# A mixed attention layer on one core: the first unit of every two in three softmax pairs is transposed by VectorE's 32x32 squares and a trip through DRAM

## The chip, the core and the metric

The kernel runs on one core of one Trainium2 chip. A core has five engines with an instruction queue each: PE (TensorE, matmuls, with its weight loads shown as PEld), DVE (VectorE), ACT (ScalarE), POOL (GpSimd) and SP (SyncE, which here only issues DMAs). Each engine works through its own queue in order; an instruction whose inputs are not there holds everything behind it on that engine. The metric is the device time of one execution in microseconds (us). Data lie in SBUF (128 partitions), matmuls write to PSUM banks, and DRAM holds inputs, outputs and a few scratch arrays.

## What is computed

A layer of a sequence model, 1024 positions by 1024 channels in float32: a layer norm with a modulation computed from a conditioning vector, one input projection, two groups of eight attention heads (stick-breaking and softmax with a forget gate), a gate, an output projection, and a residual with a second layer norm. The softmax group is the one that the change touches:

```python
s = jnp.einsum('bhqd,bhkd->bhqk', q, k) * scale
s = s + (f_q[..., :, None] - f_k[..., None, :])
s = jnp.where(causal, s, -jnp.inf)
p = jax.nn.softmax(s, axis=-1)
out = jnp.einsum('bhqk,bhkd->bhqd', p, v)
...
y = jnp.concatenate([y_fox * silu(fg), y_sb * silu(sg)], axis=-1) @ w_out
x = layer_norm(alpha * x + gate * y) * ln_g + ln_b
```

Queries go in blocks of 128; block i sees keys 0 to 128(i+1). The f_k are running sums of log forget gates, one row of 1024 for each head.

## The kernel before

**Precision.** Matmul operands are kept as a high part (rounded) and a low part (the rest), and a product is made of several matmuls (high by high, high by low, low by high). So each operand has a cast that makes the high part and a subtraction that makes the low part.

**Pairs and units.** The 16 heads go in 8 pairs p: 0 to 3 stick-breaking, 4 to 7 softmax. A unit (p, h, i) is one block of 128 queries of head h of pair p. Pairs 4 to 6 run head 0 and then head 1, each with i = 7 down to 0, so an odd i comes first of every two that share a product. Unit names in the profile and in the instruction order: `a_0_7` is the attention tile of head 0, i = 7 of the pair then running, `S_0_7` its scores, `T_0_7_0` and `T_0_7_1` its transposes for blocks 0 to 3 and 4 to 7, `pv_0_3` the product of units 7 and 6 with the values, `pt_4_0_3_0` a transposed operand of pair 4, head 0, pair of units 3, blocks 0 to 3.

**One softmax unit.** PE makes the scores S in the one S tile of PSUM (L427, L428). DVE adds the forget row `fb` and takes the row maximum in one pass, writing tile `a` (L434), which frees S. ACT takes the exponential and its row sum `l` (L440), DVE the reciprocal of `l` (L441), POOL scales `a` by it (L442). Two units later (LAG = 2) `att_transpose` turns the unit's 128x128 blocks on PE into a PSUM tile T (L478, i + 1 blocks), ACT casts T into the high part of `pt` (L480) and DVE subtracts for the low part (L481). One turn after the second unit of a pair of units has been transposed, `att_pv` makes the product on PE, 2i + 2 matmuls for odd i (L493): first all with the high part, then those with the low part, blocks 0 to 3 ahead of blocks 4 to 7. ACT, DVE and POOL then copy, add and gate the result (L512 to L514), and SP writes it to `y_dr` (L522).

**Beside it.** Between the attention matmuls of a pair, PE runs the projections of later pairs (L270 to L272, and values L327 to L329). Their weights come by SP from DRAM (L121) and are split on POOL: cast L125, subtraction L126 (`whi`, `wlo`). The output weights go the same way in pairs 4 to 6 (L123, then L125, L126), are written to `wo_dr` by SP (L830, L831), and are read back near the end (`woh`, `wol`, L821, L822), as is the gated output (`yr`, L859). Forget rows of 1024, the same on all partitions, come by ACT's DMA queue (`fb`, L391). Tiles `a` and `fb` share a pool of six SBUF buffers ("att").

**What sets the order.** PE's order is the order of the program text, written by hand: for each step k of the main loop the scores of unit k, some projection steps, a product that is ready, the transposes of unit k - 2, more projection steps. The order on ACT, DVE, POOL and SP is made by the scheduler at build time from its own estimate of times. The helper `through_dram` and the names `on_dma`, `quartered` and `squares` exist only after the change.

Of the kernel before, what the change touches and what calls it, by code (L numbers as in the profile page):

```python
# [13 lines left out]
P = 128  # L14
# [13 lines left out]
def tile_hybrid_layer(  # L28
# [82 lines left out]
    f_dr = dr.tile([8, SEQ], F32, tag="f_dr", name="f_dr")  # L111

# [132 lines left out]
    def evac_k(p, ch, acc, kst, klo, heads):  # L245
        s = slice(ch * 512, ch * 512 + 512)
        for h in heads:
            r = slice(h * HD, h * HD + HD)
            o = slice((1 - h) * HD, (1 - h) * HD + HD)
            first = nc.scalar.copy(kst[h][r, s], acc[r, :])  # L250
            kf = kst[h].bitcast(F32)
            nc.sync.dma_start(kf[o, s], kf[r, s])
            if p not in CASTS_FIRST:
                last = nc.vector.tensor_tensor(klo[r, s], acc[r, :], kf[r, s], op=ALU.subtract)
        if p in CASTS_FIRST:
            for h in heads:
                r = slice(h * HD, h * HD + HD)
                last = nc.vector.tensor_tensor(klo[r, s], acc[r, :], kst[h].bitcast(F32)[r, s], op=ALU.subtract)  # L258
        return first, last
# [106 lines left out]
    def forget_rows(lf):  # L366
# [17 lines left out]
        nc.sync.dma_start(f_dr.rearrange("h (t p) -> (h t) p", p=P), fr)  # L384
# [22 lines left out]
    def att_causal(u):  # L407
        p, h, i = u
        if p >= 4:
            f = fb[2 * (p - 4) + h]  # L410
            dg = slice(i * P, i * P + P)
            nc.vector.tensor_tensor(f[:, dg], f[:, dg], ps_causal[0][:, :P] if ps_causal else causal, op=ALU.add)

    def att_scores(u, following):
# [4 lines left out]
        w = ke // ns  # L419
        qs = slice(i * P, i * P + P)  # L420
# [3 lines left out]
        S = s_tile(f"S_{p}_{h}_{i}")  # L424
        for s in range(ns):
            ks = slice(s * w, s * w + w)
            nc.tensor.matmul(S[:, s, :w], qst[p][h][:, qs], kst[p][h][:, ks], start=True, stop=False)  # L427
            nc.tensor.matmul(S[:, s, :w], z, klo[p][:, ks], start=False, stop=True)  # L428
        v3 = lambda a: a[:, :ke].rearrange("p (a b) -> p a b", a=ns)
        if p >= 4:  # L430
# [3 lines left out]
            rows = nc.vector.tensor_tensor_reduce(out=v3(a), in0=S[:, :ns, :w], in1=v3(f),  # L434
# [7 lines left out]
            nc.gpsimd.tensor_scalar(a[:, :ke], a[:, :ke], l, 1.0, op0=ALU.mult, op1=ALU.mult)  # L442
            st_w[u] = a
        else:
# [17 lines left out]
            nc.gpsimd.memset(be[:, ke - 1:ke], 0.0)  # L462
            st_w[u] = be

    def att_transpose(u):
        p, h, i = u
        a = st_w.pop(u)
        j, qo = i // 2, (i % 2) * P
        for g in range((i // 4) + 1):
            n = min(4, i + 1 - 4 * g)  # L470
            if (p, h, j, g) not in st_pt:
                st_pt[p, h, j, g] = [pt_tile(x, f"pt{x}_{p}_{h}_{j}_{g}", F32R, [P, 4, 256])
                                     for x in range(2)]
            hi, lo = st_pt[p, h, j, g]
            tp = t_tile(f"T_{p}_{h}_{i}_{g}")
            for b in range(n):
                kb = 4 * g + b
                nc.tensor.transpose(tp[:, b * P:(b + 1) * P], a[:, kb * P:(kb + 1) * P], ident)  # L478
            t3 = tp[:, :n * P].rearrange("p (a b) -> p a b", a=n)
            nc.scalar.copy(hi[:, :n, qo:qo + P], t3)  # L480
            nc.vector.tensor_tensor(lo[:, :n, qo:qo + P], t3, hi.bitcast(F32)[:, :n, qo:qo + P],  # L481
                                    op=ALU.subtract)
# [521 lines left out]
    for k in range(len(units) + LAG + 1):  # L1004
        if k < len(units):
# [13 lines left out]
            if 4 <= p < NPAIR - 1 and i == 0:  # L1019
                load_fb(2 * (p - 4) + h + 2)  # L1020
# [3 lines left out]
        if LAG <= k < len(units) + LAG:  # L1024
            u = units[k - LAG]
            att_transpose(u)
            seen.add(u)
            if (u[0], u[1], u[2] ^ 1) in seen:
# [76 lines left out]
```

## Time and profile before

| | |
|---|---|
| time, 3 runs | 685.13 us median (685.02 to 685.16) |
| the profiled execution | 685.25 us, span 683.5 us |
| granted TensorE clock | 0.999 |
| pairs 4 to 6 | about 349 to 559 us of the span |
| DMA moved | 81.60 MB |

The profile gives, for each engine, the time in which it was busy, and the chain of work that ended last, followed back from the end. Groups of instructions are given by line, engine, operation, output and inputs, with count, busy time, and mean ns of one after the bar. A window's row gives the busy time of each engine in a stretch of the span, then the granted clock, the share of the DMA engines and GB/s. A row of the timeline is start, duration, engine, line, operation, and in brackets the idle time just before it and what ended that. In the window views a row like `x16` is a run of 16 instructions. Matmuls overlap in PE's pipeline, so their rows are longer than the step from one to the next.

### The profile page before, as it was taken

Reading aid. Unit: us, or ns where it says so; the run is one execution under the profiler, and the core shown is the slowest. Engines: PE = TensorE matmul, PEld = TensorE weight load, DVE = VectorE, ACT = ScalarE, POOL = GpSimd, SP = SyncE. Lnnn points to the kernel's source line nnn. Section 1 sums busy time; section 2 is a strip of 40 time slices with the busy share of each in tenths; the row PEclk is TensorE's granted clock in tenths of the full one; section 3 lists DMA queues with packets and bytes.
Section 4 is the critical chain, followed back from the end, with each engine's and each line's share of the span. In section 5 each row is a group of like instructions: output and inputs, shape, how many; then the busy total and the mean of one; then the engine's idle time right before and its main releaser. Section 6 shows DMA issues by size and latency. Waiting matters only on the chain.

```text
span 683.5 us, 11770 instructions
## 1 busy us (share of the span) xinstructions
PE 667.2 (98%) x4021; PEld 587.2 (86%) x4021; DVE 450.6 (66%) x914; ACT 382.0 (56%) x861; POOL 427.7 (63%) x558
## 2 busy tenths in 40 slices
PE   5999999999999999999999999999999999999995
PEld 4789898888998888889988888899988889888885
DVE  6785368867666667676675665765566677774645
ACT  5668357856567666566675564655565667531000
POOL 5558977756348566556388896877584364665411
PEclk9999999999999999999999999999999999999999
DMA  9966231112102121122144563453341298143301
GB/s 338 410 236 233 82 105 44 41 29 60 29 9 86 27 57 54 37 55 55 55 131 136 172 176 121 143 166 129 101 150 40 72 327 318 58 162 118 123 31 62
DMA packets 45036, 81.60 MB, mean 119 GB/s; under 512 B 5232, under 2 KB 18864, under 8 KB 44976
## 3 DMA queue, kind: packets, MB, share of 16 engines
q1 hardware_dynamic: 43536, 76.63, 33.8%
q10 hardware_dynamic: 1440, 4.21, 2.2%
q8 instruction: 32, 0.52, 0.3%
q14 instruction: 28, 0.23, 0.1%
HBM read 60.34 MB, written 16.29 MB: 112 GB/s over the span
## 4 chain that ended last, share of the span: by engine, by line
PE 94%; DMA 3%; DVE 2%; ACT 0%; issue 0%; POOL 0%; DVEq 0%
PE m L270 10%; PE m L272 10%; PE m L271 10%; PE pv L493 10%; PE T L478 9%; PE S L428 5%; PE S L427 5%; PE o L884 4%; PE o L882 4%; PE o L883 4%; PE v L327 4%; PE v L328 4%; PE v L329 4%; DMA raws<-in_w_qkg_dram 2%; PE st_late L589 1%; PE st_q L589 1%
## 5 line engine op out<-in xcount | busy, mean ns | idle before, releaser
L270 PE MATMUL m<-uh,whi 128*128 128x512 f32 x304 | 126.4, 416 | 0.0
L272 PE MATMUL m<-uh,wlo 128*128 128x512 f32 x304 | 119.7, 394 | 0.0
L271 PE MATMUL m<-ul,whi 128*128 128x512 f32 x304 | 119.7, 394 | 0.0
L481 DVE TENSOR_TENSOR pt<-T,pt 128x512 fp32r<-128x512 f32 (+2 forms) x192 | 100.5, 550 | 17.5 <-ACT pt L480 16.5
L461 POOL TENSOR_TENSOR be<-be,kp 128x127 f32<-128x127 f32 (+3 forms) x64 | 77.2, 1207 | 33.1 <-DVE kp L457 23.5
L480 ACT CAST pt<-T 128x512 fp32r<-128x512 f32 (+2 forms) x192 | 85.8, 480 | 16.1 <-PE T L478 12.5
L453 DVE TENSOR_TENSOR_SCAN kp<-kp,floor 128x512 f32<-128x512 f32 (+2 forms) x64 | 65.2, 1018 | 31.2 <-ACT kp L447 30.1
L493 PEld LDWEIGHTS pv<-pt,v 128*128 128x128 f32 (+1 forms) x640 | 77.1, 163 | 4.4 <-DVE pt L481 0.7
L493 PE MATMUL pv<-pt,v 128*128 128x256 f32 (+3 forms) x640 | 80.4, 271 | 0.5 <-DVE pt L481 0.5
L442 POOL TENSOR_SCALAR a<-a,l 128x1024 f32<-128x1024 f32 (+3 forms) x64 | 48.1, 751 | 40.3 <-DVE l L441 26.7
L272 PEld LDWEIGHTS m<-uh,wlo 128*128 128x128 f32 x304 | 57.1, 188 | 13.6
L440 ACT ACTIVATE a<-a,nm 128x1024 f32<-128x1024 f32 (+3 forms) x64 | 49.8, 778 | 33.8 <-DVE nm L434 32.7
L427 PE MATMUL S<-k,q 128*128 128x512 f32 (+5 forms) x192 | 66.5, 348 | 0.2 <-DVE nm L434 0.2
L428 PE MATMUL S<-kl,qz 128*128 128x512 f32 (+5 forms) x192 | 65.5, 342 | 0.0
L270 PEld LDWEIGHTS m<-uh,whi 128*128 128x128 f32 x304 | 57.3, 188 | 8.5 <-DVE kl L258 0.2
L271 PEld LDWEIGHTS m<-ul,whi 128*128 128x128 f32 x304 | 57.4, 189 | 8.0
L434 DVE CUSTOM_DVE_ANT_0 a<-S,fb 128x1024 f32<-128x1024 f32 (+3 forms) x64 | 48.3, 755 | 20.1 <-PE S L428 9.3
L514 POOL TENSOR_TENSOR ty<-ty,sg 64x256 f32<-64x256 f32 x64 | 47.5, 742 | 22.3 <-DVE ty L513 11.1
L447 ACT ACTIVATE kp<-S 128x128 f32<-128x128 f32 (+3 forms) x64 | 41.7, 652 | 31.6 <-PE S L428 29.4
L327 PE MATMUL v<-whi_v,uh 128*128 128x256 f32 (+1 forms) x192 | 56.0, 292 | 0.0
L405 ACT CAST qz<-q 64x128 fp32r<-64x128 f32 x128 | 37.4, 295 | 33.2 <-PE S L428 31.8
L328 PE MATMUL v<-whi_v,ul 128*128 128x256 f32 (+1 forms) x192 | 54.2, 282 | 0.0
(285 smaller groups left out, 1593.6 us busy)
## 6 DMA issues: line engine op xcount, KB each, us to landing
raw<-in_w_qkg_dram SPq DMA_DIRECT2D x38, 256.0 KB, 2.9
wss<-in_w_ss_dram SPq DMA_DIRECT2D x16, 512.0 KB, 8.4
x<-in_x_dram SPq DMA_DIRECT2D x8, 512.0 KB, 6.9
k<-k SPq DMA_DIRECT2D x32, 128.0 KB, 2.3
wg<-in_w_gate_dram SPq DMA_DIRECT2D x8, 512.0 KB, 4.9
raw_o<-in_w_out_dram SPq DMA_DIRECT2D x16, 256.0 KB, 2.8
fb<-f_dr ACTq DMA_DIRECT2D x8, 512.0 KB, 4.3
wo_dr<-whi_o SPq DMA_DIRECT2D x16, 256.0 KB, 2.5
```

The source lines that it names most:

```text
L270: nc.tensor.matmul(acc, hi[:, c], u_hi[kt][:, s], start=(kt == 0), stop=False)
L271: nc.tensor.matmul(acc, hi[:, c], u_lo[kt][:, s], start=False, stop=False)
L272: nc.tensor.matmul(acc, lo[:, c], u_hi[kt][:, s], start=False, stop=(kt == NB - 1))
L327: nc.tensor.matmul(acc[:, :n], u_hi[kt][:, ts_], hi[:, s], start=(kt == 0), stop=False)
L328: nc.tensor.matmul(acc[:, :n], u_lo[kt][:, ts_], hi[:, s], start=False, stop=False)
L427: nc.tensor.matmul(S[:, s, :w], qst[p][h][:, qs], kst[p][h][:, ks], start=True, stop=False)
L428: nc.tensor.matmul(S[:, s, :w], z, klo[p][:, ks], start=False, stop=True)
L453: scan = nc.vector.tensor_tensor_scan(rv, rv, floor[0][:, 512 - n:][:, ::-1], initial=0.0, op0=ALU.mult, op1=ALU.max)
L461: nc.gpsimd.tensor_tensor(be[:, :ke - 1], be[:, :ke - 1], kp[:, 1:ke], op=ALU.mult)
L480: nc.scalar.copy(hi[:, :n, qo:qo + P], t3)
L481: nc.vector.tensor_tensor(lo[:, :n, qo:qo + P], t3, hi.bitcast(F32)[:, :n, qo:qo + P], op=ALU.subtract)
L493: nc.tensor.matmul(acc[:m, q0:256], vt[p][:, kb, h * P:h * P + m], pt[:, kb % 4, q0:], start=start, stop=stop)
```

## The change

24 units, those of pairs 4 to 6 with odd i, are no longer transposed on PE. In their place:

- The scale by 1/l moves from POOL (L442) to ACT.
- DVE transposes every 32x32 square of the tile in place within its partitions, writing a new tile `squares` of the same six buffers, with the squares grouped so that each group of 32 partitions holds runs of (i + 1) x 32 elements.
- SP writes `squares` to DRAM (`far`), and four DMAs read it back into tile `a`, 32 partitions each, which puts the squares into their places.
- The split of a moved unit happens at the transposition of its partner, one unit later than before: the cast stays on ACT, with an SBUF input, and the subtraction moves from DVE to POOL.
- The forget row of the next head is loaded at the first unit of a head, one unit later than before.

`quartered` always returns False, so the code under it is not run. The diff, cut to what runs:

```diff
+    def on_dma(u):
+        p, h, i = u
+        return 4 <= p < NPAIR - 1 and i % 2 == 1
...
-            nc.gpsimd.tensor_scalar(a[:, :ke], a[:, :ke], l, 1.0, op0=ALU.mult, op1=ALU.mult)
+            if moved:
+                nc.scalar.activation(a[:, :ke], a[:, :ke], AF.Copy, scale=l)
+                squares = att_tile(f"sq_{p}_{h}_{i}")
+                nc.vector.transpose(by_blocks(squares, i + 1, False), by_blocks(a, i + 1, True))
+                through_dram(u, squares, a)
+            else:
+                nc.gpsimd.tensor_scalar(a[:, :ke], a[:, :ke], l, 1.0, op0=ALU.mult, op1=ALU.mult)
...
+    def through_dram(u, src, dst):
+        p, h, i = u
+        ke, run = (i + 1) * P, (i + 1) * 32
+        far = dr.tile([P, SEQ], F32, tag="far", bufs=4, name=f"far_{p}_{h}_{i}")
+        nc.sync.dma_start(far[:, :ke], src[:, :ke])
+        for s in range(4):
+            nc.sync.dma_start(dst[s * 32:s * 32 + 32, :ke].rearrange("k (q r) -> k q r", q=4),
+                              far[:, s * run:s * run + run].rearrange("(q k) r -> k q r", q=4))
...
     def att_transpose(u):
...
+            if on_dma(u):
+                full = a[:, :(i + 1) * P].rearrange("p (q k c) -> p k q c", q=4, c=32)[:, 4 * g:4 * g + n]
+                parts = [t[:, :n, qo:qo + P].rearrange("p k (q c) -> p k q c", q=4)
+                         for t in (hi, hi.bitcast(F32), lo)]
+                nc.scalar.copy(parts[0], full)
+                eng = nc.gpsimd if p >= 4 or g else nc.vector
+                eng.tensor_tensor(parts[2], full, parts[1], op=ALU.subtract)
+                continue
...
-            if 4 <= p < NPAIR - 1 and i == 0:
-                load_fb(2 * (p - 4) + h + 2)
+            if k > 64 and i == NB - 1 and units[k - 1][2] == 0 and 2 * (p - 4) + h + 1 < 8:
+                load_fb(2 * (p - 4) + h + 1)
...
-            att_transpose(u)
+            other = (u[0], u[1], u[2] ^ 1)
+            if not on_dma(u):
+                att_transpose(u)
+                if on_dma(other):
+                    att_transpose(other)
```

Lines after the change: scores L474 and L475, scale on POOL L498, PE's transposes L558, the moved subtraction L550, PV L573, gate L594, far write L529, reads L531, weight splits L138 and L139, projections L297 to L299.

**PE at the first units of pair 4.** The instruction order on PE before, from the last product of pair 3 (`pv_1_3`) to the next scores; `m_2_0` is a projection, `T_0_7` the transposes of unit (4,0,7):

```order
L493 MATMUL pv_1_3_4350<-pt_3_1_3_1_4258,v_1979 128x256
L478 MATMUL T_0_7_0_4374<-ident,a_0_7_4214 128x128 x4
L478 MATMUL T_0_7_1_4383<-ident,a_0_7_4214 128x128 x4
L270 MATMUL m_2_0_4328<-uh_116,whi_2_1_4196 128x512
L271 MATMUL m_2_0_4328<-ul_124,whi_2_1_4196 128x512
L272 MATMUL m_2_0_4328<-uh_116,wlo_2_1_4197 128x512
```

The same place on PE after, and a little later the transposes of the partner and the first product of pair 4, which takes the moved unit's parts (`pt_4_0_3_0_4417` and `pt_4_0_3_1_4426` are low parts):

```order
L573 MATMUL pv_1_3_4366<-pt_3_1_3_1_4266,v_1979 128x256
...
L558 MATMUL T_0_6_0_4418<-ident,a_0_6_4285 128x128 x4
L558 MATMUL T_0_6_1_4427<-ident,a_0_6_4285 128x128 x3
L474 MATMUL S_0_3_4449<-k_0_3502,q_0_3290 128x512
...
L573 MATMUL pv_0_3_4487<-pt_4_0_3_0_4416,v_3710 128x256 x4
L573 MATMUL pv_0_3_4487<-pt_4_0_3_1_4425,v_3710 128x256 x2
L573 MATMUL pv_0_3_4487<-pt_4_0_3_1_4425,v_3710 128x128
L573 MATMUL pv_0_3_4487<-pt_4_0_3_0_4417,v_3710 64x256 x4
L573 MATMUL pv_0_3_4487<-pt_4_0_3_1_4426,v_3710 64x256 x2
```

The eight transposes of the odd unit are gone; those of the even unit, the scores and the product keep their order.

**POOL at the same place.** Before (`raw_o`, `whi_o`, `wlo_o` are output weights, `ty` a gate, `a_0_5` and `a_0_4` scales):

```order
L123 TENSOR_TENSOR raw_o_0_4464<-raw_o_0_4464,gate 128x512
L442 TENSOR_SCALAR a_0_5_4319<-a_0_5_4319,l_0_5_4321 128x768
L125 TENSOR_SCALAR whi_o_0_4467<-raw_o_0_4464 128x512
L123 TENSOR_TENSOR raw_o_1_4608<-raw_o_1_4608,gate 128x512
L514 TENSOR_TENSOR ty_1_3_4367<-ty_1_3_4367,sg_3101 64x256
L126 TENSOR_TENSOR wlo_o_0_4468<-raw_o_0_4464,whi_o_0_4467 128x512
L125 TENSOR_SCALAR whi_o_1_4611<-raw_o_1_4608 128x512
L442 TENSOR_SCALAR a_0_4_4401<-a_0_4_4401,l_0_4_4403 128x640
L126 TENSOR_TENSOR wlo_o_1_4612<-raw_o_1_4608,whi_o_1_4611 128x512
```

After:

```order
L136 TENSOR_TENSOR raw_o_0_4478<-raw_o_0_4478,gate 128x512
L550 TENSOR_TENSOR pt_4_0_3_0_4417<-a_0_7_4214,pt_4_0_3_0_4416 128x4x128
L138 TENSOR_SCALAR whi_o_0_4481<-raw_o_0_4478 128x512
L594 TENSOR_TENSOR ty_1_3_4383<-ty_1_3_4383,sg_3101 64x256
L136 TENSOR_TENSOR raw_o_1_4613<-raw_o_1_4613,gate 128x512
L139 TENSOR_TENSOR wlo_o_0_4482<-raw_o_0_4478,whi_o_0_4481 128x512
L138 TENSOR_SCALAR whi_o_1_4616<-raw_o_1_4613 128x512
L498 TENSOR_SCALAR a_0_4_4399<-a_0_4_4399,l_0_4_4401 128x640
L550 TENSOR_TENSOR pt_4_0_3_1_4426<-a_0_7_4214,pt_4_0_3_1_4425 128x4x128
L139 TENSOR_TENSOR wlo_o_1_4617<-raw_o_1_4613,whi_o_1_4616 128x512
```

The first of the two subtractions of unit (4,0,7) stands where the scale of (4,0,5) stood; the second stands behind the scale of (4,0,4).

**SP at the end of pair 6.** Before (`y_dr` is a gated output written, `yr` one read back, `xr` the residual input, `woh` and `wol` output weights read back):

```order
L859 DMA yr_4_7196<-y_dr 128x3x128
L894 DMA xr_7478<-in_x_dram 128x1024
L822 DMA wol_6814<-wo_dr 128x1024
L821 DMA woh_6813<-wo_dr 128x1024
L522 DMA y_dr<-ty_1_2_6776 64x256
L822 DMA wol_6830<-wo_dr 128x1024
L821 DMA woh_6829<-wo_dr 128x1024
L859 DMA yr_0_7316<-y_dr 128x4x128
```

After, with the trip of unit (6,1,1):

```order
L939 DMA yr_4_7232<-y_dr 128x3x128
L974 DMA xr_7514<-in_x_dram 128x1024
L901 DMA woh_6846<-wo_dr 128x1024
L529 DMA far_1_1_6788<-sq_1_1_6786 128x256
L902 DMA wol_6847<-wo_dr 128x1024
L902 DMA wol_6867<-wo_dr 128x1024
L901 DMA woh_6866<-wo_dr 128x1024
L939 DMA yr_0_7352<-y_dr 128x4x128
L602 DMA y_dr<-ty_1_2_6820 64x256
L531 DMA a_1_1_6778<-far_1_1_6788 32x4x64 x4
```

The far write stands behind the first of the `woh` loads, its reads behind three more such loads and a `yr`.

More of the change, by code (lines that the diff above doesn't have):

```diff
@@ L249, in evac_k @@
             o = slice((1 - h) * HD, (1 - h) * HD + HD)
-            first = nc.scalar.copy(kst[h][r, s], acc[r, :])
             kf = kst[h].bitcast(F32)
-            nc.sync.dma_start(kf[o, s], kf[r, s])
+            first = nc.scalar.copy(home(kst[h], r), made(acc, r))
+            if quartered(p):
+                both = [kf[x, :].rearrange("p (s z) -> p s z", s=4)[:, :, ch * P:ch * P + P] for x in (o, r)]
+                nc.sync.dma_start(*both)
+            else:
+                nc.sync.dma_start(kf[o, s], kf[r, s])
             if p not in CASTS_FIRST:
-                last = nc.vector.tensor_tensor(klo[r, s], acc[r, :], kf[r, s], op=ALU.subtract)
+                last = nc.vector.tensor_tensor(home(klo, r), made(acc, r), home(kf, r), op=ALU.subtract)
         if p in CASTS_FIRST:
@@ L383, in forget_rows @@
         nc.scalar.copy(fr, ft)
-        nc.sync.dma_start(f_dr.rearrange("h (t p) -> (h t) p", p=P), fr)
+        if quartered(4):
+            for hh in range(8):
+                nc.sync.dma_start(f_dr[hh].rearrange("(s t c) -> t s c", s=4, c=32),
+                                  fr[8 * hh:8 * hh + 8, :].rearrange("t (s c) -> t s c", s=4))
+        else:
+            nc.sync.dma_start(f_dr.rearrange("h (t p) -> (h t) p", p=P), fr)
         yield
@@ L419, in att_scores @@
         w = ke // ns
+        moved = on_dma(u)
+        quarters = quartered(p)
+        run = (i + 1) * 32
         qs = slice(i * P, i * P + P)
@@ L433, in att_scores @@
             l = sb.tile([P, 1], F32, tag="l", bufs=4, name=f"l_{p}_{h}_{i}")
[L434 removed]
+            ends = v3(a), S[:, :ns, :w], v3(f)
+            if quarters:
+                ends = by_quarter(a[:, :ke]), S4, by_quarter(f)[:, :, :run]
+            rows = nc.vector.tensor_tensor_reduce(out=ends[0], in0=ends[1], in1=ends[2],
                                            op0=ALU.add, op1=ALU.min, scale=-1.0, scalar=BIG,
```

42 lines of the change are left out of this document (36 added, 6 removed).

## Prediction

> **What bounds the kernel now.** I read the page's busy times first, then the chain of work that ended last, then two stretches of the softmax pairs.
>
> ```profile
> PE 667.2 (98%) x4021; PEld 587.2 (86%) x4021; DVE 450.6 (66%) x914; ACT 382.0 (56%) x861; POOL 427.7 (63%) x558
> PE 94%; DMA 3%; DVE 2%; ACT 0%; issue 0%; POOL 0%; DVEq 0%
> core 0: us, PE busy (x) PEld busy (x) DVE busy (x) ACT busy (x) POOL busy (x), PEclk, DMA share, GB/s
> 358.00:438.00 80.00, 80.00 (x456) 69.25 (x455) 48.24 (x123) 43.93 (x106) 66.98 (x75) 1.00 0.49 153
> 438.00:558.00 120.00, 119.74 (x779) 107.57 (x778) 77.34 (x210) 69.97 (x177) 75.21 (x90) 1.00 0.41 126
> ```
>
> PE is busy for 98% of the span and holds 94% of the chain; the granted clock is 1.00 in both stretches. So work taken off PE pays in full, unless something makes PE wait. The reader is to see POOL as well: 67 of 80 us in the first stretch (pair 4), 75 of 120 in the second (pairs 5 and 6).
>
> **The gain.** 24 units (odd i, pairs 4 to 6) lose their PE transposes: 8+6+4+2 = 20 blocks a head, 120 in all. What one occupies is read where eight stand in a row:
>
> ```profile
> 359.94 1.94 PE L493 MATMUL pv<-pt,v 128*128 128x256 f32 x16
> 361.72 1.04 PE L478 MATMUL T<-ident,a 128*128 128x128 f32 x8
> 362.51 0.48 PE L270 MATMUL m<-uh,whi 128*128 128x512 f32 x1
> 362.83 0.40 PE L271 MATMUL m<-ul,whi 128*128 128x512 f32 x1
> 363.06 0.40 PE L272 MATMUL m<-uh,wlo 128*128 128x512 f32 x1
> ```
>
> L271 to L272 is one step of the pipeline, 0.23 us; L270 would have started its step at 362.83 - 0.23 = 362.60, and 362.60 - 361.72 = 0.88 us for eight, 0.110 each. 120 x 0.110 = **13.2 us** (2.2 a head), and this is the value I take. The row's own 1.04 us, 0.130 each, counts the drain of the pipeline as well and would give 15.6, the upper end; what falls short of 13.2 is a wait, and those are counted below.
>
> The Trainium skill, page "VectorE: DVE Perf Modes", section "The three transpose paths", gives a 128x128 bf16 transpose 390 ns on TensorE and 311 on VectorE, there in 32x32 blocks only, and its section "Rules for kernel authors" says to use TensorE where the result may go to PSUM, which speaks against this change. By 390 ns the gain would be 46.8 us; the trace's step of 110 ns disagrees, for f32 and a filled pipeline, and decides.
>
> **What moves on the other engines,** per head, with ke = 1024, 768, 512, 256 for i = 7, 5, 3, 1:
>
> ```profile
> L442 POOL TENSOR_SCALAR a<-a,l 128x1024 f32<-128x1024 f32 x8 | 9.0, 1130 | 5.1 <-DVE l L441 5.1
> L442 POOL TENSOR_SCALAR a<-a,l 128x256 f32<-128x256 f32 x8 | 3.9, 487 | 6.1 <-DVE l L441 3.2 <-PE v L329 2.8
> L126 POOL TENSOR_TENSOR wlo<-raw,whi 128x512 fp32r<-128x512 f32 x38 | 49.1, 1297 | 2.4 <-DMA wo_dr<-wlo_o 0.8
> L514 POOL TENSOR_TENSOR ty<-ty,sg 64x256 f32<-64x256 f32 x64 | 47.5, 742 | 22.3 <-DVE ty L513 11.1 <-issue 4.7 <-PE v L328 1.7
> L440 ACT ACTIVATE a<-a,nm 128x1024 f32<-128x1024 f32 x8 | 9.2, 1152 | 6.4 <-DVE nm L434 6.4
> L440 ACT ACTIVATE a<-a,nm 128x256 f32<-128x256 f32 x8 | 4.1, 511 | 4.9 <-DVE nm L434 4.8
> L434 DVE CUSTOM_DVE_ANT_0 a<-S,fb 128x1024 f32<-128x1024 f32 x8 | 9.7, 1216 | 2.1 <-PE S L428 2.1
> L434 DVE CUSTOM_DVE_ANT_0 a<-S,fb 128x256 f32<-128x256 f32 x8 | 3.4, 423 | 3.3 <-issue 2.2 <-PE S L428 1.2
> L481 DVE TENSOR_TENSOR pt<-T,pt 128x512 fp32r<-128x512 f32 x96 | 64.6, 686 | 16.8 <-ACT pt L480 16.3
> L481 DVE TENSOR_TENSOR pt<-T,pt 128x256 fp32r<-128x256 f32 x32 | 13.3, 415 | 0.2
> L480 ACT CAST pt<-T 128x512 fp32r<-128x512 f32 x96 | 54.8, 587 | 7.7 <-PE T L478 5.0
> ```
>
> ACT takes the scale, four sizes from 1.152 to 0.511 us, on the line through these 2 x (1.152 + 0.511) = 3.33 us a head. Its share of the first stretch goes from 43.9 to about 52 of 75 us: no bound. DVE loses four 512-wide and two 256-wide subtractions, 4 x 0.686 + 2 x 0.415 = 3.57, and gains four transposes in squares, which no row shows. By the nearest row (L434, same elements, one pass) they are 2 x (1.216 + 0.423) = 3.28; free would be 0, two passes 6.56. I take 3.28: about even. With two passes DVE is at 48.2 - 7.1 + 13.1 = 54 of 75 us, so its busy time bounds nothing.
>
> **POOL** loses the scales, 2 x (1.130 + 0.487) = 3.23 a head, and gains four 512-wide subtractions at 1.297 and two 256-wide at L514's 0.742, 6.67 a head. In the first stretch: both heads' subtractions +13.34; the scales -6.46, except the first one, which lies before it, +1.13; the first unit of pair 5 2 x 1.297 - 1.130 = +1.46. That is 66.98 + 9.5 = **76.5 us of POOL**, against a stretch of PE work that shrinks to 80 - 2 x 2.2 - 0.88 = **74.7 us**. POOL cannot keep pace there, and its new rows stand on PE's path. The first of them:
>
> ```profile
> 368.80 0.80 POOL L442 TENSOR_SCALAR a<-a,l 128x640 f32<-128x640 f32 x1
> 368.60 1.18 PE L493 MATMUL pv<-pt,v 128*128 128x256 f32 x9
> ```
>
> The scale of unit (4,0,4) ended at 369.60. In the new order a 1.30 subtraction stands ahead of it in the place of a 0.93 scale (+0.37), and the second subtraction of unit (4,0,7) behind it (+1.30): 371.27. Its product stands twelfth of 16 in PV (1.94 us for 16 above, 0.12 each), at 368.60 + 11 x 0.12 - 0.88 = 369.0: a stall of 2.2 us at the first unit already. By the bare excess the stretch loses 76.5 - 74.7 = 1.8; if POOL keeps half of its present 13 us of idle time, it is 76.5 + 6.5 = 83.0 long and loses 8.3. I take the middle, the whole 5.3 us of gain. **+5.3, from 1.8 to 8.3.** In the second stretch POOL gets 75.2 + 12.4 = 87.6 of 112 us: enough.
>
> **The round trip,** in the second stretch. The window runs from the row sums (L434) of the odd unit to PV of its pair; below, (5,0,7), (6,1,7) and (6,1,1):
>
> ```profile
> 420.68 1.22 DVE L434 CUSTOM_DVE_ANT_0 a<-S,fb 128x1024 f32<-128x1024 f32 x1
> 438.37 1.85 PE L493 MATMUL pv<-pt,v 128*128 128x256 f32 x15
> 522.91 1.23 DVE L434 CUSTOM_DVE_ANT_0 a<-S,fb 128x1024 f32<-128x1024 f32 x1 [0.86 <-PE S L428]
> 538.73 1.54 PE L493 MATMUL pv<-pt,v 128*128 128x256 f32 x12
> 546.79 0.42 DVE L434 CUSTOM_DVE_ANT_0 a<-S,fb 128x256 f32<-128x256 f32 x1 [0.32 <-issue]
> 559.73 0.78 PE L493 MATMUL pv<-pt,v 128*128 128x256 f32 x4
> L440 ACT ACTIVATION_READ_ACCUMULATOR a<-a,nm 128x1 f32 x64 | 12.0, 187 | 0.0
> L441 DVE RECIPROCAL l<-l 128x1 f32<-128x1 f32 x64 | 10.4, 162 | 25.6 <-ACT a L440 24.4 <-POOL wlo L126 0.3 <-POOL whi_o L125 0.3
> k<-k SPq DMA_DIRECT2D x32, 128.0 KB, 2.3
> wo_dr<-whi_o SPq DMA_DIRECT2D x16, 256.0 KB, 2.5
> fb<-f_dr ACTq DMA_DIRECT2D x8, 512.0 KB, 4.3
> woh<-wo_dr SPq DMA_DIRECT2D x8, 512.0 KB, 8.2
> 559.20 0.37 SPq L859 DMA_DIRECT2D yr<-y_dr  x1
> 548.00:558.00 10.00, 10.00 (x55) 8.31 (x54) 7.14 (x19) 6.02 (x15) 6.91 (x10) 1.00 0.92 301
> ```
>
> For i = 7: row sums 1.23, exp 1.15 + 0.19, reciprocal 0.16, scale 1.15, squares 1.22, issue 0.37, the 512 KB write 3.0 (between 2.5 for 256 KB and 4.3 for fb), four read issues 1.5, the last 128 KB landing 2.3: 12.3 us. Then a cast 0.59 and two subtractions 2.6: 15.5. The window of (6,1,7) is 15.8 - 0.9 saved + 1.3 into PV = 16.2. One POOL row of 1.3 ahead in its queue and it stalls 0.6 (squares in two passes would add 1.2); that of (5,0,7) is 1.9 wider. I take **+1.5 for pairs 5 and 6, from 0 to 5.**
>
> **Buffers.** The squares share the six attention buffers, so that in DVE's new order seven row sums (which free the one S bank) wait until the squares before them have been written out. The first such pair, and PE's next S:
>
> ```profile
> 357.42 0.95 DVE L434 CUSTOM_DVE_ANT_0 a<-S,fb 128x768 f32<-128x768 f32 x1
> 364.79 0.82 DVE L434 CUSTOM_DVE_ANT_0 a<-S,fb 128x640 f32<-128x640 f32 x1 [0.52 <-PE S L428]
> 366.65 0.47 PE L427 MATMUL S<-k,q 128*128 128x512 f32 x1
> ```
>
> With exp and scale at 0.94 each (768 wide, a third of the way down between L440's two rows) and squares at 0.95: 357.42 + 0.95 + 0.94 + 0.19 + 0.16 + 0.94 + 0.95 + 0.37 + 2.5 = 364.4: it lands just before the row sums need it, and 366.65 - 365.61 = 1.0 us lies behind them. With queueing of a microsecond each, half of it hidden by that: **+0.5, from 0 to 3**.
>
> At the end of pair 6, i = 1: row sums to squares 0.42 + 0.51 + 0.19 + 0.16 + 0.51 + 0.42 = 2.2, write 0.37 + 2.3, reads 1.5 + 2.3, cast and subtraction at most 1.9: 10.6 of 12.9 us. But DMA is full there (share 0.92) and the write now stands on SP behind a woh load, the reads behind three more and a yr. With one leg at woh's 8.2 the trip is 16.5 and PV is 3.6 late; less 0.6, as the subtraction is one of 256. **+3, from 0 (neither leg) to 9 (both).** The last forget row, loaded one unit later, would land in that same stretch and adds nothing to it; the earlier rows still have a whole head between load and use.
>
> SP also holds weight loads behind the reads, which wait for the far copy to land, and POOL holds weight splits behind its new rows. I cost this at nothing: the cover is that PE was busy 80.00 of 80.00 us in the first stretch, ahead of which POOL's splits run; without it each would cost about one POOL row, 1.3 us.
>
> **Sum,** against the profiled run's own 685.25: 685.25 - 13.2 + 5.3 + 1.5 + 0.5 + 3.0 = 682.35. That run lies 0.1 above the median of 685.13, so **682.3**.
>
> **Rivals.** (1) A clean win: POOL's lag stays off PE and the trips fit: 685.1 - 13.2 = 672, up to 676 with small stalls. For it: PE never waited in the first stretch before. Against: 76.5 of 74.7 us. (2) Nothing changes, 683.8 to 686.5: pair 4 costs 8.3, the rest stays, or the end costs 6: the gain is used up by POOL's queue and the full DMA. (3) **Slower: the landing wait in ACT's queue.** The cast of a moved unit waits on ACT for four landings; behind it in order stand the copy of q for the next S and the next exp, which hold DVE, then PE. It decides once a trip is longer than its window, about 16 us for i = 7. With the write at fb's 4.3 and the reads at 4.3 too, the trip is 3.3 longer, 18.8 with cast and subtractions, 2.6 past the window: six units of i = 7 lose 2.6 each; those of i = 5, whose trip is some 2 shorter, 0.6 each: 19.2 us, of which pair 4's third hides in POOL's loss and 1.5 is counted: 682.3 + 12.8 - 1.5 = 694, or 688 if half is caught up. Against: the 128 KB landings took 2.3. (4) The change not doing what it says is excluded by the order: the 120 transposes are gone from PE.
>
> **How the numbers follow.** My sum, spread by its terms (678 to 685), 0.52; clean win 0.14; used up 0.14; slower 0.20, from 687 to 694. A measurement tells about 0.2% (1.4 us) from no change: below 683.7 is faster, above 686.5 slower. The sum's case gives faster 0.40, same 0.08, slower 0.04. Together faster 0.54, same 0.21, slower 0.25. The range leaves out half of the clean win's chance and the worst of the slower case: 674.5 to 691.
>
> **What would show it.** Right: in the first stretch PE idle ended by POOL, POOL above 95%, the stretch no shorter than before; in the second a few waits of PV for the moved subtractions; a gap near PV (6,1,0). Wrong: PE above 99% in the first stretch (then 676 and below); or ACT idle before the moved casts, put down to DMA, with DVE and PE behind it all along (then 690 and above); squares far dearer than 1.2 us.

## The result, and the profile after

The changed kernel takes 709.9 us (median of 4 runs, 706.8 to 710.3) against 685.1 (685.0 to 685.2) before: **slower, ratio 1.035, 95% interval 1.032 to 1.038**. The forecast was 682.3, from 674.5 to 691. The profiled execution took 710.2 us, span 708.5.

Busy times and chain of the page after, then the two stretches shown of before:

```profile
PE 667.7 (94%) x3901; PEld 582.0 (82%) x3901; DVE 447.7 (63%) x902; ACT 399.2 (56%) x885; POOL 446.1 (63%) x570
PE 69%; DMA 12%; DVE 5%; ACT 4%; issue 3%; POOL 3%; SPq 2%; ACTq 0%; DVEq 0%; POOLq 0%
```

```profile
358.00:438.00 80.00, 72.99 (x379) 61.74 (x378) 43.99 (x110) 46.50 (x106) 66.00 (x71) 0.96 0.64 203
438.00:558.00 120.00, 108.57 (x661) 94.77 (x660) 68.32 (x185) 74.16 (x176) 84.70 (x92) 0.97 0.60 186
```

PE has 120 instructions less and is no less busy; it holds 69% of the chain, and the DMA's share rose from 3 to 12%. PE now stands still in both stretches, and **the granted clock fell to 0.96 and 0.97**, which no term of the prediction had. POOL, at 66 of 80 us, is not full.

Whom PE waited for in the whole span (us in total, times, longest), and the two waits of DVE and ACT for the trip; the first line is PE's wait for row sums before the change:

```profile
PE S L427 <- DVE nm L434: 0.2, 1, 0.2
PE S L474 <- DVE nm L484: 13.4, 6, 3.6
PE pv L573 <- ACT pt L548: 6.0, 2, 4.0
PE v L354 <- DVE v L363: 3.0, 2, 1.5
PE pv L573 <- POOL pt L550: 2.2, 4, 0.8
DVE a L484 <- DMA far<-sq: 12.2, 6, 3.9
ACT pt L548 <- DMA a<-far: 38.3, 21, 4.6
```

The largest is the wait for row sums on DVE, which free the S bank. Followed back in the trace one by one, the six waits of 13.4 us divide: one (3.38) goes back to row sums that waited for the far write, four (3.62, 3.12, 1.94 and 0.78) to a moved cast on ACT that waited for the reads, and one (0.60) plainly to neither. PE's waits for POOL, where the forecast had its largest loss, are 2.2 us. The first gap shows the wait for the write, by the timeline of SP, DVE and PE, and one window of 4 us (its clock is third from the right):

```profile
364.34 0.35 SPq L134 DMA_DIRECT2D raw_o<-in_w_out_dram  x1
364.79 0.38 SPq L529 DMA_DIRECT2D far<-sq  x1
371.13 0.82 DVE L484 CUSTOM_DVE_ANT_0 a<-S,fb 128x640 f32<-128x640 f32 x1 [3.92 <-DMA far<-sq]
367.72 0.93 PE L558 MATMUL T<-ident,a 128*128 128x128 f32 x7
372.02 0.71 PE L474 MATMUL S<-k,q 128*128 128x512 f32 x1 [3.38 <-DVE nm L484]
372.95 0.63 PE L297 MATMUL m<-uh,whi 128*128 128x512 f32 x1
373.38 0.63 PE L298 MATMUL m<-ul,whi 128*128 128x512 f32 x1
377.31 0.39 PE L297 MATMUL m<-uh,whi 128*128 128x512 f32 x1
377.54 0.40 PE L298 MATMUL m<-ul,whi 128*128 128x512 f32 x1
```

```profile
372.00:376.00 4.00, 3.98 (x12) 3.21 (x13) 3.00 (x9) 4.00 (x10) 2.12 (x3) 0.57 0.63 184
```

The write of unit (4,0,5) is issued at 364.79 and the row sums of the next unit, which reuse its squares' buffer, start at 371.13; PE's next S waits 3.38 us. Behind that gap a projection matmul takes a step of 373.38 - 372.95 = 0.43 us; at 377 it is 0.23 again. The window's clock, 0.57, says the same: after the standstill PE ran at half rate for some 3.5 us, which costs another (1 - 0.57) x 4 = 1.7 us.

The gap at 447.57 shows the other wait, in ACT's queue:

```profile
444.82 0.62 ACT L548 CAST pt<-a 128x512 fp32r<-128x512 f32 x1 [2.20 <-DMA a<-far]
445.35 0.58 ACT L254 ACTIVATE q<-m 64x512 fp32r<-64x512 f32 x1
445.96 0.69 DVE L255 SCALAR_TENSOR_TENSOR q<-m,q 64x512 fp32r<-64x512 f32 x1 [3.74 <-ACT q L254]
446.68 0.82 DVE L484 CUSTOM_DVE_ANT_0 a<-S,fb 128x640 f32<-128x640 f32 x1
447.57 0.79 PE L474 MATMUL S<-k,q 128*128 128x512 f32 x1 [3.12 <-DVE nm L484]
```

The cast stands on ACT until the reads have landed, and the next activation (a later pair's projected q, L254) is behind it; DVE waits 3.74 us for that one with the row sums behind it, and PE waits 3.12 us for the row sums.

How late each place of the program is against before (start of the row sums of its first unit on DVE, us; the last column is the fourth unit of pair 7, behind the trip of unit (6,1,1)):

| kernel | pair 4 | pair 5 | pair 6 | pair 7 | (7,1,6) |
|---|---|---|---|---|---|
| before, at | 348.8 | 420.7 | 490.8 | 552.8 | 563.7 |
| changed | +2.6 | +8.9 | +14.5 | +19.2 | +25.2 |
| no_trip | 0.0 | +2.2 | +3.2 | +0.1 | +1.3 |
| no_trip_dve | -0.2 | -1.9 | -1.2 | -3.9 | -3.1 |
| unwaited | -0.3 | +1.4 | +10.6 | +12.4 | +11.9 |
| small | +1.4 | +3.8 | +12.8 | +14.6 | +24.4 |
| small_own | -0.2 | +3.4 | +8.0 | +8.5 | +18.2 |
| held_small_own | -0.2 | +5.4 | +6.6 | +10.8 | +20.8 |

The 2.6 us ahead of pair 4 lie before anything that the change touches: this execution had a clock of 0.69 between 10 and 20 us of its span, where the profile of before had 1.00. So the change cost 25.0 - 2.6 = 22.4 us in it, of which 6.3 in pair 4, 10.3 in pairs 5 and 6, and 6.0 at the end; with the 13.2 that PE was spared, 35.6 us were lost. PE's gaps between 340 and 600 us add up to 25.2 us (0.2 before), and the slow clock behind five of them to about 8.6 by windows of 4 us; the remaining 2 us I put down to the 15 stops themselves: a 512-wide row lasts 0.39 us and its step 0.23, and a gap is counted from the end of the row, so by estimate a stop costs 0.16 us more than its gap.

### The profile page after: what moved, and what is told of

It is laid out like the page before. It is cut to its first block, busy times and chain, and to the rows that moved or that the text cites. A ratio compares the mean times of both kernels' runs of the same rounds, so it can differ in the third digit from the quotient of the medians.

```text
span 708.5 us, 11843 instructions
## 1 busy us (share of the span) xinstructions
PE 667.7 (94%) x3901; PEld 582.0 (82%) x3901; DVE 447.7 (63%) x902; ACT 399.2 (56%) x885; POOL 446.1 (63%) x570
## 4 chain that ended last, share of the span: by engine, by line
PE 69%; DMA 12%; DVE 5%; ACT 4%; issue 3%; POOL 3%; SPq 2%; ACTq 0%; DVEq 0%; POOLq 0%
PE pv L573 7%; PE m L297 6%; PE m L298 6%; PE m L299 6%; PE T L558 5%; PE o L964 4%; PE o L962 4%; PE o L963 4%; DMA far<-sq 4%; DMA a<-far 4%; PE S L474 3%; PE S L475 3%; PE v L354 3%; PE v L356 3%; PE v L355 3%
## 5 line engine op out<-in xcount | busy, mean ns | idle before, releaser
L297 PE MATMUL m<-uh,whi 128*128 128x512 f32 x304 | 126.9, 417 | 0.4 <-DVE kl L284 0.4
L299 PE MATMUL m<-uh,wlo 128*128 128x512 f32 x304 | 120.8, 397 | 0.0
L573 PE MATMUL pv<-pt,v 128*128 128x256 f32 (+3 forms) x640 | 82.6, 274 | 8.8 <-ACT pt L548 6.0
L573 PEld LDWEIGHTS pv<-pt,v 128*128 128x128 f32 (+1 forms) x640 | 77.8, 164 | 14.7 <-ACT pt L548 6.8
L561 DVE TENSOR_TENSOR pt<-T,pt 128x512 fp32r<-128x512 f32 (+3 forms) x156 | 80.5, 539 | 11.2 <-ACT pt L560 10.0
L560 ACT CAST pt<-T 128x512 fp32r<-128x512 f32 (+3 forms) x156 | 69.4, 471 | 24.9 <-PE T L558 22.0
L474 PE MATMUL S<-k,q 128*128 128x512 f32 (+5 forms) x192 | 67.8, 355 | 13.4 <-DVE nm L484 13.4
L299 PEld LDWEIGHTS m<-uh,wlo 128*128 128x128 f32 x304 | 58.1, 191 | 14.0
L484 DVE CUSTOM_DVE_ANT_0 a<-S,fb 128x1024 f32<-128x1024 f32 (+3 forms) x64 | 48.1, 752 | 30.4 <-DMA far<-sq 12.2
L475 PE MATMUL S<-kl,qz 128*128 128x512 f32 (+5 forms) x192 | 66.4, 347 | 0.0
L297 PEld LDWEIGHTS m<-uh,whi 128*128 128x128 f32 x304 | 58.5, 192 | 9.5 <-DVE kl L284 0.9
L594 POOL TENSOR_TENSOR ty<-ty,sg 64x256 f32<-64x256 f32 x64 | 47.4, 741 | 22.9 <-DVE ty L593 11.2
L356 PE MATMUL v<-wlo_v,uh 128*128 128x256 f32 (+1 forms) x192 | 54.1, 282 | 0.0
L474 PEld LDWEIGHTS S<-k,q 128*128 128x128 f32 x192 | 36.4, 190 | 20.7 <-DVE nm L484 15.6
```

What stands on the lines that cost most here:

```text
L297: nc.tensor.matmul(acc, hi[:, c], u_hi[kt][:, s], start=(kt == 0), stop=False)
L299: nc.tensor.matmul(acc, lo[:, c], u_hi[kt][:, s], start=False, stop=(kt == NB - 1))
L356: nc.tensor.matmul(acc[:, :n], u_hi[kt][:, ts_], lo[:, s], start=False, stop=(kt == NB - 1))
L474: nc.tensor.matmul(sp, qst[p][h][:, qs], kh, start=True, stop=False)
L475: nc.tensor.matmul(sp, z, kl, start=False, stop=True)
L573: nc.tensor.matmul(acc[:m, q0:256], vt[p][:, kb, h * P:h * P + m], pt[:, kb % 4, q0:], start=start, stop=stop)
```

## The experiments

One run each unless said otherwise. The kernel before took 685.3, 686.8, 685.2, 686.8 and 685.1 us beside the five groups of runs, and a start like that above can move a run by some 2 us.

### Taking the trip apart

**no_trip** leaves the trip out; **unwaited** sends it, to nowhere; **write_only** and **reads_only** keep one leg.

```diff
-                through_dram(u, squares, a)
+                a = squares                       # no_trip
+                through_dram(u, squares, a)       # unwaited, reads go to DRAM: back[...] <- far[...]
+                a = squares
+                # write_only: through_dram without the four reads
+                # reads_only: without the far write, reads take x[:P, ...]
```

> Leaves out the far write and the four reads; the moved units' split reads the squares directly, so these units' blocks are not fully transposed. All instructions on PE, DVE, ACT and POOL stay. Theory 1 (PE's 25 us of gaps come from waits for the trip's landings): the gaps go, 672 to 678 us, granted clock back at 0.99 or more. Rival (POOL's 36 new subtractions, 76.5 us of POOL work in the stretch of pair 4, are what PE waits for): 684 us or more, with PE waiting for POOL in pair 4.

Measured 686.4. The trip is what makes the kernel slow (709.9 to 686.4), and yet **without it nothing is gained**: 13.2 us spared, 14.3 lost (span 684.7 against 683.5). PE's waits, and in the timeline of POOL and PE the place that the prediction worked out by hand:

```profile
PE pv L573 <- POOL pt L550: 7.0, 4, 2.8
PE v L354 <- DVE v L363: 1.5, 1, 1.5
```

```profile
369.36 1.26 POOL L550 TENSOR_TENSOR pt<-sq,pt 128x512 fp32r<-128x512 f32 x1
371.18 1.29 POOL L550 TENSOR_TENSOR pt<-sq,pt 128x512 fp32r<-128x512 f32 x1
370.68 0.75 PE L573 MATMUL pv<-pt,v 128*64 128x256 f32 x5 [1.52 <-POOL pt L550]
```

The rival was the better forecast of the number, and POOL is what PE waits for, though one of the waits (2.1 us, at 443 us) lies in pair 5.

> The far write and four reads are still issued with the same sizes, but the reads land in another DRAM array and the split reads the squares, so no engine but SP waits for a landing; results of the moved units are not fully transposed. Theory 1 (waits for landings): 672 to 680 us. Rival (the traffic itself: 15.7 MB more on the DMA engines and SP's queue delay weights and other loads): 690 us or more.

Measured 698.3, as its rival had it: but for 1.6 us on ACT, no engine other than SP waits for a landing of the trip, and still 11.9 us more than no_trip. The waits of SP, POOL and PE, and three rows of the timeline of POOL and PE, name the way:

```profile
SPq L533 <- DMA far<-sq: 28.6, 18, 4.5
POOL raw_o L136 <- DMA raw_o<-in_w_out_dram: 14.6, 8, 3.2
PE pv L575 <- POOL pt L552: 13.1, 5, 3.6
```

```profile
481.48 1.26 POOL L136 TENSOR_TENSOR raw_o<-raw_o,gate 128x512 f32<-128x512 f32 x1 [3.25 <-DMA raw_o<-in_w_out_dram]
484.07 1.26 POOL L552 TENSOR_TENSOR pt<-sq,pt 128x512 fp32r<-128x512 f32 x1
485.38 1.23 PE L575 MATMUL pv<-pt,v 128*64 128x256 f32 x5 [3.61 <-POOL pt L552]
```

SP stands 28.6 us in front of the reads until the write has landed; the weight loads behind are issued late; POOL, in order, stands before a weight product (between 350 and 570 us of the span 14.6 us here, 1.0 in no_trip, 9.4 before the change) and with it the subtraction that PE needs, with two rows between them. None of PE's waits is for the weights themselves.

> Keeps the squares and the far write, leaves out the four reads; the split takes the tile untransposed. So the cast on ACT waits for no landing, but the squares' buffers still come free only when the write has landed. If the buffers (row sums that wait for the far write) carry the loss: 685 to 695 us, with DVE waits for far as in the changed kernel (12 us). If the cast's wait in ACT's queue carries it: 674 to 680 us.

> Leaves out the far write; the four reads take rows of the input x and overwrite the tile as soon as the squares are made, so moved units hold other data. The cast on ACT still waits for four landings, about 4 us earlier than in the changed kernel, and no buffer waits for a write. If the write leg makes the trip too long (by itself or by the buffers): 672 to 680 us. If four read landings on ACT's queue are enough to stall: 690 us or more.

Measured 688.9 and 691.1 (reads_only's reads go out earlier, as nothing is to land first). Each leg alone costs 2 to 5 us over no_trip, both together 23: the legs are not additive. In write_only DVE waits 17.6 us for the far write and PE 7.9 us for row sums, with none for the cast, as its first forecast had it. In reads_only ACT waits 12.7 us for the reads and PE 3.9 us for row sums and 7.2 for POOL; 691.1 is just inside its second forecast.

### POOL's subtractions

```diff
-                eng = nc.gpsimd if p >= 4 or g else nc.vector
+                eng = nc.vector                   # no_trip_dve (without the trip), dve_sub (with it)
```

> As no_trip (no far write, no reads, blocks not fully transposed), and the 36 subtractions of the moved units are on DVE as before the change. Theory (in no_trip the 7 us of PE waits for POOL's subtractions, and the slow clock behind them, eat the gain of 13.2 us): the waits for POOL go, 674 to 679 us. Rival (the 120 transposes were worth less than 13.2 us, or the other edits take it): 683 us or more with POOL's waits gone.

Measured 682.1 beside 686.8 for before, clock 0.998: the waits for POOL and the slow clock go. So having the subtractions on POOL costs about 4.4 us of span (684.7 to 680.2) where there is no trip, and by the table nearly all of it arises in pair 4. But of 13.2 us still only 3.3 arrive, and 682.1 lies between the two forecasts. PE's waits are now small and many:

```profile
PE S L474 <- DVE nm L484: 2.6, 4, 0.9
PE v L354 <- DVE v L363: 2.0, 1, 2.0
PE pv L573 <- DVE pt L561: 1.7, 4, 0.6
PE T L558 <- POOL a L498: 1.3, 1, 1.3
```

Between 340 and 600 us PE's gaps add up to 7.6 us; before had 0.2. I read them as waits that PE's transposes had covered, as the chains on ACT, DVE and POOL for each unit have not become shorter; no run separates this from the other edits.

> The whole change, with the 36 subtractions of the moved units on DVE in place of POOL. If POOL's queue is a cause beside the trip: 10 us less than the changed kernel, 698 to 702 us. If the trip's landings set PE's gaps and POOL's queue only lies in their shadow: 705 to 712 us.

Measured 714.9, no better than the changed kernel and above both forecasts: PE waits 17.4 us for row sums there (13.4 in the changed kernel). With the trip, POOL's rows lie in its shadow.

### The clock

```diff
+                if (t, h, pr) == (2, 0, 3):       # in the kernel before, between two output tiles
+                    for _ in range(7):            # gap_short; 9 in gap_long
+                        nc.scalar.copy(wo[3][0], wo[3][0].bitcast(F32))
```

> The kernel before with 7 in-place copies of one output weight tile on ACT between two output tiles, so that PE stands still once for about 2 us; the outputs are the same. If only a long standstill lowers the granted clock: 2 to 3 us more than before and no slow matmuls. If every standstill does: 1.8 us more on top.

> The same with 9 copies: one standstill of about 4.5 us. If the standstill halves the clock for about 3.5 us behind it: its length plus 1.5 to 2 us, with 512-wide matmuls at a step of 0.43 us in place of 0.23. If the clock doesn't depend on it: its length alone.

Measured 689.1 and 692.7 (686.8 before). PE's rows behind the standstill, gap_short first:

```profile
637.57 0.50 PE L882 MATMUL o<-woh,whi_y 128*128 128x512 f32 x1 [2.90 <-ACT woh L940]
637.91 0.39 PE L883 MATMUL o<-woh,wlo_y 128*128 128x512 f32 x1
638.14 0.39 PE L884 MATMUL o<-wol,whi_y 128*128 128x512 f32 x1
```

```profile
638.76 0.80 PE L882 MATMUL o<-woh,whi_y 128*128 128x512 f32 x1 [5.05 <-ACT woh L940]
639.35 0.63 PE L883 MATMUL o<-woh,wlo_y 128*128 128x512 f32 x1
639.78 0.63 PE L884 MATMUL o<-wol,whi_y 128*128 128x512 f32 x1
```

After 2.90 us the step stays 0.23; after 5.05 us it is 0.43 for 12 matmuls, which is 12 x 0.20 = 2.4 us. The spans, 687.4 and 691.0, agree: they are 3.6 us apart, and gap_short had already started 1.0 us later (its clock was 0.83 between 10 and 20 us, 1.00 in gap_long), so from the standstill on the difference is 4.6, of which 2.15 is the longer gap and about 2.4 the clock. So a gap costs its length here, and where the clock falls behind it 1.7 us (the first gap above) to 2.4 us more. gap_short did what its first forecast says; gap_long's clock cost more than the 1.5 to 2 us forecast.

### Where the wait for the trip is held

**late_fb** loads forget rows at i = 2 of the head before; **late_split** splits a moved unit one unit later and its product too; **late_both_dve** does both and subtracts on DVE; **small** moves only i = 3 and 1.

```diff
-                if on_dma(other):
-                    att_transpose(other)
+                if on_dma(other):
+                    held.append(other)            # late_split: split at the next step, PV after that
...
-        return 4 <= p < NPAIR - 1 and i % 2 == 1
+        return 4 <= p < NPAIR - 1 and i % 2 == 1 and i < 4                    # small
```

> The whole change, but each forget row is loaded six units later (at i = 2 of the head before), so that for most of a head five of the six attention buffers, not four, hold tiles and squares. If buffers that wait for the far write to land carry the loss: DVE's wait for far (12 us) falls by half or more and the time to 698 us or less. If the cast's wait for the reads in ACT's queue carries it: 705 us or more.

> The whole change, but the moved unit is split one unit later still, and its product comes one unit later, so that the cast on ACT asks for the landings some 4 to 5 us later. ACT waited 38 us for them in 21 casts, 1.8 each. If that wait in ACT's queue carries the loss: ACT's wait for the reads nearly goes, 690 us or less. If the buffers carry it (tiles now live longer in the same six): 705 us or more.

> Only the moved units of i = 3 and i = 1 stay moved (12 of 24 units, 36 of 120 blocks, worth 4.0 us of PE); i = 7 and 5 are as before the change. Their trips were 7.7 to 12.6 us up to the cast, against 13 to 18 for i = 7 and 5. If long trips carry the loss: 681 to 685 us and no slow clock. If any trip does (buffers, ACT's queue): 690 us or more.

> The whole change with the split one unit later, the forget rows six units later, and the subtraction on DVE: the three suspected waits are loosened together. If they are the whole cause: 676 to 684 us, granted clock 0.99 or more. If the trip's traffic on SP and the DMA engines holds something else: 695 us or more.

Measured 720.5, 710.0, 709.6 and 706.6: none came near the time that one of these causes alone would give, nor did all three loosened together. late_fb cut DVE's wait for the far write from 12.2 to 1.2 us, but ACT's wait for the reads rose to 50.0. late_split left that wait at 37.6, and small has nearly as much with half of the trips, the short ones (37.3 us in 10 casts). The instruction order on ACT explains it: between a unit's scale and its first cast lie 7 to 15 instructions in the trace of the changed kernel, 6 to 16 in late_split, 6 to 14 in small. So the later place in the program text did not move the cast; I take it that the scheduler puts it where, by its own estimate, the data have landed.

**held, held_late, held_small, held_late_dve** fix the cast's place:

```diff
-                nc.scalar.copy(parts[0], full)
+                with after(*hold):                # the newest exponential and copy of q in the text
+                    nc.scalar.copy(parts[0], full)
```

> The whole change, and the cast of a moved unit must stand on ACT behind the exponential and the copy of q that the program text has ahead of it, so that its wait holds neither the next scores nor the next row sums. Trips and traffic are the same. If the place of the cast in ACT's queue is the cause: ACT's wait for the reads falls from 38 us to under 12, 688 to 696 us. If the trips' traffic or buffers are: 705 us or more.

> As held, with the split and the product one unit later, so that the cast stands 17 to 26 rows behind the scale. If the place of the cast is the whole cause: near the kernel without the trip (686), 684 to 690 us, ACT's wait for the reads under 5 us. If buffers carry a part: 692 to 700 us with DVE waits for far. If traffic does: 705 us or more.

> Only i = 3 and 1 moved, with the cast held as in held. If the place of the cast is the cause: 681 to 686 us (709.6 without the hold). If not: 700 us or more.

> As held_late with the moved subtractions on DVE. If both POOL's queue and the cast's place are the causes, this comes near the kernel without trip and without POOL's subtractions (682): 680 to 685 us.

Measured 725.4, 717.8, 711.2 and 716.7. The cast now stands 13 to 23 instructions behind the scale in held, 16 to 27 in held_late, and ACT's wait for the reads is nearly gone (2.1 us in held, 3.9 in held_small, none in the other two). The time did not fall: in held DVE waits 34.5 us for the far write (17 times; 12.2 before the hold), its squares wait 13.4 us for POOL to release a tile, and PE waits 26.1 us for the moved subtractions. That theory fell too. The wait only moved; as I read it, a tile that is split later frees its buffer later, and with six buffers the next row sums then hang on the write instead.

**small_own, held_small_own** take the buffers away as well: for i = 3 and 1 the squares fit into the unused half of the unit's own tile.

```diff
-                squares = att_tile(f"sq_{p}_{h}_{i}")
+                squares = a[:, ke:2 * ke]         # with i < 4 only
```

> Only i = 3 and 1 moved, and their squares written to the unused half of the unit's own tile, so that no other tile waits for the far write; the cast's place is the scheduler's, as in small (709.6). If the two waits are both causes: the far wait on DVE goes, ACT's wait for the reads stays, 690 to 705 us. If buffers alone: 681 to 686.

> The same with the cast held back as in held_small (711.2). If the two waits are the whole cause, both are gone and the gain of 36 blocks, 4 us, less some waits shows: 680 to 686 us. If the trip costs by something else (traffic, SP, tiles that live a unit longer): 695 us or more.

Measured 703.7, with ACT's wait for the reads still 32.0 us, as forecast for two causes; and 708.5 (four runs, ratio 1.034, interval 1.032 to 1.036), where the gain was to show. In held_small_own DVE's wait for the far write is gone and ACT's for the reads is left once (3.8 us, at the last unit). What PE waits for is now the moved subtraction:

```profile
PE pv L575 <- POOL pt L552: 11.3, 8, 2.6
PE pv L575 <- ACT pt L550: 6.7, 2, 6.2
```

Only the longest of these, 6.2 us, is a wait for a landing: it belongs to unit (6,1,1). In the other eleven units the reads had landed 0.9 to 8.1 us before the held cast began, and the subtraction behind it came late in POOL's queue. So there the wait is for the place that the hold gave the cast and for POOL, and no longer for the trip; the same kernel with the subtractions on DVE was not run.

Some 10 us of both kernels are a single place, the trip of unit (6,1,1) (last two columns of the table). In the changed kernel it reads, on SP, ACT and PE:

```profile
568.53 0.38 SPq L901 DMA_DIRECT2D woh<-wo_dr  x1
570.37 0.32 SPq L529 DMA_DIRECT2D far<-sq  x1
570.75 0.96 SPq L902 DMA_DIRECT2D wol<-wo_dr  x2
574.99 4.57 SPq L531 DMA_DIRECT2D a<-far  x4
582.38 0.41 ACT L548 CAST pt<-a 128x256 fp32r<-128x256 f32 x1 [4.56 <-DMA a<-far]
582.84 0.44 PE L573 MATMUL pv<-pt,v 128*128 128x256 f32 x2 [4.02 <-ACT pt L548]
```

The four reads take 4.57 us to be issued alone (1.75 at the first unit), as SP waits for the loads of output weights between them, and the trip lasts from 570.37 to the cast at 582.38. No run that computes the layer beat the kernel before.

## Why the prediction was wrong, by its steps

- **The gain, 13.2 us,** fits the runs: no_trip_dve's span is 3.3 us shorter with 7.6 us of new gaps, and ten stops at 0.16 us make 1.6 more, 12.5 in all. What was wrong is the step from PE's 98% to work that "pays in full": the rest of a unit's chain was not ready earlier, so part of the time taken off PE came back as waits, 9.9 us of it without any trip and with the moved subtractions on DVE. The sum has no term for this.
- **POOL, +5.3 (1.8 to 8.3):** the mechanism was right at its first place (stall foreseen 2.2, measured 1.52 in no_trip), and its size, 4.4 us by no_trip against no_trip_dve, is in the range and falls in pair 4 (3.9 us by the table's first two columns). In the changed kernel it lies in the shadow of the trip.
- **The round trip, +1.5 (0 to 5), and the buffers, +0.5 (0 to 3): the step that failed.** Up to the start of pair 7 the changed kernel lost 16.5 us more than no_trip, which has the same work without the trip; the sum had 2.0 for it. Pairs 5 and 6 came out 10.3 us later where the sum had them 5.9 earlier. Two things were wrong. First the size, by the median landings after:

```profile
far<-sq SPq DMA_DIRECT2D x6, 512.0 KB, 3.4
a<-far SPq DMA_DIRECT2D x24, 128.0 KB, 3.5
far<-sq SPq DMA_DIRECT2D x6, 384.0 KB, 4.3
a<-far SPq DMA_DIRECT2D x24, 96.0 KB, 2.4
```

  I took 3.0 and 2.3 for i = 7 from other transfers of the kernel before, at a lower DMA share (0.49 and 0.41 in the two stretches; 0.64 and 0.60 after), and 2.5 for the write of i = 5, which took 4.3 (6.19 at the worst). From row sums to the last landing the i = 7 trips took 12.9 to 17.9 us (12.3 foreseen), those of i = 5, which I had priced only as some 2 shorter, 11.0 to 15.8. Second and worse, the window: I compared the trip with the time until PE needs the result. The cast comes much earlier in ACT's order, with other work behind it that DVE and PE need first (the rows at 444.82 to 447.57 above), so a trip that is in good time for PE still blocks. small shows it: before its last unit PE never waits for a moved product, and yet ACT stands 37.3 us before moved casts, PE waits 9.9 us for row sums, and the 12 short trips make it as slow as all 24 (709.6, some 10 us of it at the last unit).
- **The end, +3 (0 to 9):** 6.0 measured, of which no_trip has 1.2 without any trip. The place is as written, a slow trip among the loads of output weights: the write took 4.5 us to land where 2.3 was the bare value, and the issue of the reads 4.6 where 1.5 was.
- **Weight loads held on SP, costed at nothing:** the cover that I named was the wrong one. PE never waited for the weights, but POOL's in-order queue stood at the late load with PE's subtraction behind it; unwaited, where almost nothing else waits for the trip, is 11.9 us slower than no_trip.
- **Left out: the clock.** About 8.6 us in the changed kernel, none before.
- **The rivals.** The slower one, a landing wait in ACT's queue, was the right kind (38.3 us of such waits, 21 casts), with its price of 688 to 694 too low and its point of decision wrong: I had put it at a trip longer than PE's window. The sign that the prediction gave for it, ACT idle before the moved casts with DVE and PE behind, is what the trace shows. Used up by POOL's queue describes no_trip well (686.4), and the clean win had no support in any run. (The parts of the chances add up to 0.22 for same and 0.24 for slower, not 0.21 and 0.25.)

Shown by runs: the trip as a whole costs 21 to 24 us over the same kernel without it; without it the change would gain nothing as it stands, and 3.3 us with the subtractions on DVE; a gap of 5.05 us slows the clock, one of 2.90 did not. Shown only as moved waits, and not settled as separate prices: ACT's queue, the six buffers, SP's queue and the place at the end hide behind each other, so that taking one away showed the next. In the changed kernel's own trace about 18 of PE's 25.2 us of gaps go back to a cast that waited for the reads; that says what ended last there, not what is won without it, as the held runs show. A version for the small units with the squares in their own tile, a held cast and a later product was not run, nor was one with more buffers, nor the small units without their trip.

## What to carry to other kernels

Before work is taken off a busy engine, ask of every instruction on the new path in which in-order queue it waits and what stands directly behind it there; the time until its final user is the wrong window. The trip through DRAM held something here during its whole time, a queue or a buffer, and as neither was to spare, its cost moved about and did not go. Price a transfer under the load it will meet, and a PE gap at its length plus the slow restart that may follow it (1.7 to 2.4 us here).

## What the hardware showed unexpectedly

The half rate behind a gap has no sharp bound here. Over all these traces, the start of the span left aside, no gap under 1.8 us that stood alone was followed by a half clock (shorter ones close together were, as 1.65 and 1.61 us in late_fb); of those between 1.8 and 3 us some were (2.77 us in no_trip, 1.87 in write_only) and some not (2.90 in gap_short, 2.87 in write_only); all from 3.3 us on were. By the traces' clock records the half clock lasts 3.41 us or two or three times that, except for the last stretch of each span. The Trainium skill, page "TensorE: Matmul & The Clock Gate", section "Part 1: The HAM clock gate (the "warmup" mystery)", describes two rates, 1.2 and 2.4 GHz, set by activity windows of about 3.4 us that run freely. The steps here, 0.43 and 0.23 us for 512 columns, agree with the two rates, and the mixed outcomes between 1.8 and 3 us agree with windows that run freely. The same page of the Trainium skill, section "Why this matters for your kernels", asks for no idle gaps of PE over about 3 us. Here gaps of 1.87 and 2.77 us were already followed by the half clock.
